# A hybrid decoder layer on one core: three small inputs loaded ahead of the modulation weights, the shift sum moved into a weight buffer, and one group's squares at earlier slices

## The chip, the cores and the metric

The kernel runs on one core of a Trainium2 chip. The metric is the device time of one execution in microseconds (us); lower is better. A core has five engines that run their own instruction streams side by side: TensorE (PE in the profile, with its weight loads shown apart as PEld), VectorE (DVE), ScalarE (ACT), GpSimd (POOL) and SyncE (SP). They wait for one another through semaphores. Transfers between memory and the core's buffers are issued by SP, ACT or POOL and carried out by 16 DMA engines. An instruction that waits holds up all that stands behind it on its engine, an issue of a transfer too.

## The reference

One decoder layer for 2048 tokens of width 1024. Cut to what matters here:

```
mod = silu(c) @ w_ada + b_ada              # c: 1024, w_ada: 1024 x 3072
shift, scale, gate = split(mod, 3)
h = rms_norm(x, g_pre) * (1 + scale) + shift        # x: 2048 x 1024
proj = h @ w_in
qa, ka, va, fa, za, qb, kb, vb, zb = split(proj)
oa = forgetting_attention(qa, ka, va, fa + b_fgate) * silu(za)      # 8 heads, causal
qb, kb = rope(qb, positions), rope(kb, positions)   # angle = position * inv_freq
ob = sliding_window_sink_attention(qb, kb, vb, sinks) * silu(zb)    # 8 heads, window 128
y = concat(oa, ob) @ w_out
x = x + gate * rms_norm(y, g_post)
```

Before any projection can start, the kernel needs `scale` and `shift`, that is two thirds of the product of `silu(c)` with 12 MB of `w_ada` (8 MB here), and the angles need `positions` and the 32 frequencies.

## The kernel before, in words

Tokens are worked in four groups of 512 (group `ci` = 0 to 3, `CH` = 512). A group is four x tiles of 128 rows (`xt0` to `xt15`, 512 KB each). For each tile the sum of squares is taken (`squares`, L421, on ACT for most tiles: one activation with a summing read), the inverse root for the group (`root`, L101 to L121), and the tile is scaled (`normal`, L433 on ACT for group 0, L435 on DVE for the others). `turn(ci, k)` transposes the 128 columns of slice k of a group's four tiles on PE (L441), applies scale and shift on ACT (`scaled`, L447, writes `hf` and for even k the high half), and DVE splits the result into two 16-bit halves of `hT` (`split`, L451 and L452). `hT[ci]` is the moving operand of the projections: `proj_units` (L353, keys kb, zb and others) and `vb_units` (L807). A projection's weights arrive raw (`wr_...`, L219 or L226, two buffers of tag `wraw`), and ACT and DVE turn them into a high half (`wh_...`, L271) and a low half (L277).

**The start block** (L470 to L692) is written out by hand, and its order on each engine is the order of the code. It loads `c`, `g_pre`, `b_ada`, `positions` and `inv_freq` (on ACT's queue), the 16 tiles `wa1k` (scale half) and `wa0k` (shift half) of `w_ada` (on SP's queue, L489, pool `wad` of 8 buffers), the first x tiles (L412), the raw weights `wr_kv` and `wr_zb1` (on POOL's queue) and `wr_zb0` (SP). The small rows are transposed into columns (L503, L506). The product of `silu(c)` with a half of `w_ada` is shared between PE and DVE: for most k PE multiplies a broadcast copy of `silu(c)` (`ada_pe`, L525), and for the others (1: k = 2, 4, 6; 0: k = 2, 4, 7) DVE accumulates `wa * sil` into `acc1` (scale) or `acc0` (shift) (`ada_dve`, L534 and L536), whose column sums PE adds with a matrix of ones; `ada_col` (L545) takes the diagonal out as columns. Between them, DVE computes angles for sine and cosine (`ang`, `kh`, L563 to L588), which begin with positions times `ifr`. The scaled shift and gain (`Gp`, `Shp`, L673 and L674) come last; after them the first `scaled` of group 0 can run, and with it the first projection. The rope tables are copied into place by SP (`spread`, L466 and L467), and then SP loads `xt8` and the tiles that follow.

**After the start block**, a list of units (`punits`) is emitted in order: for each group kb and vb, and for groups 0 to 2 a zb or va projection behind them. Every second unit is one slice; events bound to a slice (`at_slice`) are emitted ahead of it: the loads, squares, root and normal of the group that is two ahead, the turns of the next group (`at_` gives the places among the group's units), the weight halves. Outside the hand-ordered block, which of several independent instructions stands first on a queue is settled when the program is scheduled, not by one line of the code; the order shown below is what came out.

The lines that matter later: `wh_zb` (L271 on ACT) needs its place on ACT behind the squares of group 2; zb0's projection on PE needs `wh_zb` and its low half. The squares of group 3 stand, on ACT, ahead of the last turn's `hf` of group 2.

Of the kernel before, what the change touches and what calls it, by code (L numbers as in the profile page):

```python
# [10 lines left out]
F32 = mybir.dt.float32  # L11
# [32 lines left out]
def hybrid_layer(  # L44
# [17 lines left out]
    V, A, G, PE, SP = nc.vector, nc.scalar, nc.gpsimd, nc.tensor, nc.sync  # L62
# [20 lines left out]
    def sm(n, tag):  # L83
        return small.tile([P, n], F32, tag=tag, name=tag)
# [7 lines left out]
    def rsqrt_mean(dst, ss, n, eng=None):  # L92

        for _ in rsqrt_parts(dst, ss, n, eng=eng):
            pass
# [39 lines left out]
    wpool = right.enter_context(tc.tile_pool(name="wpool", bufs=2, side="right"))  # L135
# [19 lines left out]
    ident = const.tile([P, P], F32, name="ident")  # L155
# [26 lines left out]
    bk = [ps_bk.tile([P, CH], F32, name=f"bk{n}") for n in range(3)]  # L182
# [231 lines left out]
    def squares(ci, us=range(4), eng=None):  # L414
        if ci not in rstd:
            rstd[ci] = sm(4, "ss"), sm(4, "rst")
        for u in us:
            junk = hst.tile([P, D], BF16, tag="junk", name="junk", bufs=1)
            x_, sum_ = xt[ci * 4 + u], rstd[ci][0][:, u:u + 1]
            if eng is None:  # L420
                A.activation(junk[:], x_, AF.Square, accum_out=sum_)  # L421
            else:
                eng.scalar_tensor_tensor(junk[:], x_, 1.0, x_, op0=ALU.mult, op1=ALU.mult, accum_out=sum_)

    def root(ci):
        ss, rst = rstd[ci]
        rsqrt_mean(rst, ss[:], 4, G if ci else None)

    def normal(ci, us=range(4)):
        for u in us:  # L430
            t, r = ci * 4 + u, rstd[ci][1][:, u:u + 1]
            if ci == 0:
                A.activation(xt[t], xt[t], AF.Copy, scale=r)  # L433
            else:
                V.tensor_scalar(xt[t], xt[t], r, None, op0=ALU.mult)  # L435
# [20 lines left out]
    def turn_x(ci, k):  # L456
        scaled, split = turn(ci, k)
        after(1, scaled)
        after(2, split)

    def spread(g):

        gr, gc = slice(32 * g, 32 * g + 32), slice(g * CH, (g + 1) * CH)
        for r in range(4):
            rr = slice(32 * r, 32 * r + 32)
            SP.dma_start(cosT[rr, gc], cs_[gr, :])  # L466
            SP.dma_start(sinT[rr, gc], (sp_ if r % 2 else sn_)[gr, :])  # L467

    start = ExitStack()
    st = start.enter_context(tc.tile_pool(name="start", bufs=1, reuse_waits="tile"))  # L470
    wad = start.enter_context(tc.tile_pool(name="wad", bufs=8, reuse_waits="tile"))
    with tc.manual_schedule():
        rows = st.tile([P, P], F32, name="rows")
        posi = st.tile([4, CH], I32, name="posi")
        posf = st.tile([4, CH], F32, name="posf")
        sel = st.tile([4, 4, 32], F32, name="sel")
        ifr = st.tile([P, 1], F32, name="ifr")
        V.memset(rows[:], 0.0)
        V.memset(ones[:], 1.0)
        V.memset(lift[:], LIFT_A)  # L480
        A.dma_start(rows[0:8], c[0].rearrange("(k p) -> k p", p=P))
        A.dma_start(rows[8:16], g_pre[0].rearrange("(k p) -> k p", p=P))
        A.dma_start(rows[16:40], b_ada[0].rearrange("(k p) -> k p", p=P))
        A.dma_start(posi[:], positions[0].rearrange("(g n) -> g n", g=4))
        wa = {}

        def load_ada(half, k):
# [1 line left out]
            SP.dma_start(wa[half, k][:], w_ada0[k * P:(k + 1) * P, half * D:(half + 1) * D])  # L489


        A.dma_start(ifr[:], inv_freq)
        for k in range(KT):
            load_ada(1, k)
        for t in range(2):
# [4 lines left out]
        G.dma_start(bfg[:], b_fgate[0].partition_broadcast(P))  # L500
        V.tensor_copy(identb[:], ident[:])
        V.tensor_copy(identh[:], ident[:])
        PE.transpose(bk[0][:, :P], rows[:], ident[:])  # L503
        cols = st.tile([P, 40], F32, name="cols")
        V.tensor_copy(sel[:], ident[0:4, 0:4].unsqueeze(2).broadcast_to([4, 4, 32]))
        V.tensor_copy(cols[:], bk[0][:, :40])  # L506
        th = st.tile([P, KT], F32, name="th")
        A.activation(th[:], cols[:, 0:8], AF.Tanh, scale=0.5)
        hc = st.tile([P, KT], F32, name="hc")
        V.tensor_scalar(hc[:], cols[:, 0:8], 0.5, None, op0=ALU.mult)  # L510
# [7 lines left out]


        pm = {1: [ps_x.tile([P, CH], F32, tag="x", name="pm") for _ in range(2)], 0: [bk[1], bk[2]]}  # L520
        acc = [st.tile([P, D], F32, name=f"acc{n}") for n in range(2)]

        def ada_mm(half, lhsT, rows_, begin, end):
            for n in range(2):
                PE.matmul(pm[half][n][:], lhsT, rows_[:, n * CH:(n + 1) * CH], start=begin, stop=end)  # L525

        def ada_pe(half, k, begin=False, end=False):
            ada_mm(half, silb[:, k, :], wa[half, k], begin, end)

        def ada_dve(half, k, first_, parts=1):  # L530
            for n in range(parts):
                cc = slice(n * D // parts, (n + 1) * D // parts)
                if first_:
                    V.tensor_scalar(acc[half][:, cc], wa[half, k][:, cc], sil[:, k:k + 1], None, op0=ALU.mult)  # L534
                else:
                    V.scalar_tensor_tensor(acc[half][:, cc], wa[half, k][:, cc], sil[:, k:k + 1], acc[half][:, cc],  # L536
                                           op0=ALU.mult, op1=ALU.add)
# [25 lines left out]
        V.tensor_scalar(ang[:], bk[1][:], ifr[:], None, op0=ALU.mult)  # L563
# [26 lines left out]
        A.activation(sn_[:], sp_[:], AF.Copy, scale=-1.0)  # L590
        A.activation(dmask[:], dm32[:], AF.Copy)
        A.activation(dmaskT[:], dm32t[:], AF.Copy)

        def col8(name):
            return st.tile([P, KT], F32, name=name)


        for k in (0, 1, 3, 5, 7):
            ada_pe(1, k, k == 0)
        for k in (2, 4, 6):  # L600
            ada_dve(1, k, k == 2)
        for k in range(2):
# [25 lines left out]
        V.tensor_tensor(scl1[:], scl0[:], cols[:, 24:32], op=ALU.add)  # L628
        gcol = col8("gcol")
        V.scalar_tensor_tensor(gcol[:], scl1[:], 1.0, cols[:, 8:16], op0=ALU.add, op1=ALU.mult)  # L630
# [22 lines left out]
        shf0 = col8("shf0")  # L653
        ada_col(0, shf0)
        shf = col8("shf")
        V.tensor_tensor(shf[:], shf0[:], cols[:, 16:24], op=ALU.add)
# [315 lines left out]
    pkeys, punits = [], []  # L972
# [39 lines left out]
    def at_slice(n, f):  # L1012
        events.setdefault(n, []).append(f)
# [12 lines left out]
    for ci in range(NCH):  # L1026
        n0 = len(punits)
        add("kb", kb_units(ci))
        add("vb", vb_units(ci))
        if ci < 3:  # L1030
            add(*others[ci])
            if ci == 2:
                add(*others[4])
                add(*others[5])

            mine, punits[n0:] = punits[n0:], []
            at_ = ([14, 16, 17, 18, 19, 20, 21, 22], [8, 10, 12, 14, 16, 18, 20, 22], [18, 20, 22, 24, 26, 28, 30, 32])[ci]
            for n, u in enumerate(mine):
                punits.append(u)
                if n in at_:  # L1040
                    punits.append(lambda ci=ci, k=at_.index(n): turn_x(ci + 1, k))
            if ci < 2:

                for u in range(4):
                    at_slice(n0 + (28 if ci else 9) + u, lambda ci=ci, u=u: squares(ci + 2, (u,)))
                    at_slice(len(punits) + (10 if ci else -4) + u, lambda ci=ci, u=u: normal(ci + 2, (u,)))
                at_slice(len(punits) - (0 if ci else 18), lambda ci=ci: root(ci + 2))
            at_slice((12, 22, 30)[ci], lambda ci=ci: spread(ci + 1))
    n0 = len(punits)
    at_slice(n0, lambda: open_fox())  # L1050
# [742 lines left out]
```

## Time and profile before

| | us |
|---|---|
| median of 3 runs | 1155.18 (1154.89 to 1155.92) |
| the profiled execution | 1158.72, its span 1157.0 |
| PE busy | 1117.7 (97% of the span) |
| DVE busy | 929.3 (80%) |
| ACT busy | 660.3 (57%) |
| POOL busy | 209.1 (18%) |

The profiled execution lies 3.54 us above the median; its span leaves 1.7 us of it outside. PE is busy almost throughout, so its idle stretches and the stretches at a lower clock are where an edit of these lines can be seen. In the 40 slices of the profile (28.9 us each) PE shows 6 and 8 tenths in the first two and 9 or 10 tenths in nearly all of the others. Rows of a timeline give the start in us from the span's start, the duration, the engine (a q behind the name: its queue of waits and transfer issues), the line, the operation, output and inputs, how many instructions the row joins, and in brackets the idle time ahead of it and what ended that.

### The profile page before, as it was taken

What the parts mean: (1) busy time and instruction counts of PE and PEld (TensorE: products, weight loads), DVE (VectorE), ACT (ScalarE), POOL (GpSimd) and SP (SyncE); (2) the same over time, 40 slices, a digit from 0 to 9 for tenths busy, and PEclk for the clock granted to TensorE, in tenths of its full rate; (3) what the DMA queues carried; (4) which work ended last, traced back from release to release, by engine and by line L of the source; (5) the groups of instructions that cost most, each with busy time, mean ns of one, the idle gap of its engine ahead of it and who ended that gap; (6) DMA issues with size and microseconds to landing.
All of it is one profiled execution on the core that took longest, in us unless ns stands there. A gap on an engine that the chain in (4) does not pass through costs nothing. (4 is left out here: it accounts for less than half of the span.)

```text
span 1157.0 us, 25261 instructions
## 1 busy us (share of the span) xinstructions
PE 1117.7 (97%) x9853; PEld 654.9 (57%) x9853; DVE 929.3 (80%) x2149; ACT 660.3 (57%) x1148; POOL 209.1 (18%) x328
## 2 busy tenths in 40 slices
PE   6898999999999999999999999999999999999997
PEld 2476545577765865555555555555555555544444
DVE  6877468887878558788988899887898897778885
ACT  2776334655655521676757667666676778633332
POOL 1221124555556530010010101001000000000000
PEclk9999999999999999999999999999999999999999
DMA  9843345433232232443326332222311237687643
GB/s 341 308 127 70 79 82 100 96 58 88 61 86 94 57 82 58 63 104 49 82 61 83 90 62 59 53 49 70 53 40 36 78 92 220 138 221 204 196 142 109
DMA packets 123276, 119.84 MB, mean 104 GB/s; under 512 B 64872, under 2 KB 100752, under 8 KB 123156
## 3 DMA queue, kind: packets, MB, share of 16 engines
q1 hardware_dynamic: 112020, 85.67, 27.3%
q0 software_dynamic: 10816, 32.50, 13.3%
q8 instruction: 77, 1.26, 0.6%
q14 instruction: 43, 0.35, 0.2%
q10 hardware_dynamic: 320, 0.05, 0.0%
HBM read 64.49 MB, written 25.18 MB: 78 GB/s over the span
## 5 line engine op out<-in xcount | busy, mean ns | idle before, releaser
L1363 ACT ACTIVATE p<-sta,lift,scl_qk 128x1024 f32<-128x1024 f32 (+2 forms) x160 | 171.8, 1074 | 131.7 <-PE sta L1357 81.8
L353 PE MATMUL bk<-hT,wh_qk 128*128 128x512 f16 x768 | 194.7, 378 | 0.0
L1370 DVE TENSOR_TENSOR pha<-p,pha 128x1024 f16<-128x1024 f32 (+2 forms) x160 | 169.1, 1057 | 0.2 <-ACT pha L1367 0.2
L1310 DVE TENSOR_REDUCE a_m<-bk 128x1 f32<-128x512 f32 x192 | 130.4, 686 | 46.3 <-PE bk L1307 45.3
L1585 PE MATMUL bk<-wohl,oz 128*128 128x512 f16 x744 | 163.7, 379 | 1.1 <-DVE oz L1534 0.7
L1367 ACT ACTIVATE pha<-p 128x1024 f16<-128x1024 f32 (+2 forms) x160 | 148.1, 926 | 5.9 <-PE poa L1383 1.2
L1585 PEld LDWEIGHTS <-oz 128*128 128x128 f16 x744 | 70.6, 98 | 84.7 <-DVE oz L1534 1.8
L1383 PE MATMUL poa<-vt,pha 128*128 128x65 f16 x1088 | 116.1, 192 | 1.4 <-DVE pha L1370 1.4
L1380 PE MATMUL poa<-vt,pha 128*128 128x65 f16 x1088 | 116.6, 193 | 0.8 <-DVE ona L1389 0.7
L1382 PE MATMUL poa<-vt,pha 128*128 128x64 f16 x1088 | 116.6, 194 | 0.0
L353 PEld LDWEIGHTS <-wh_qk 128*128 128x128 f16 x768 | 72.1, 97 | 74.5 <-issue 2.1
L1356 PE MATMUL sta<-T 128*128 128x512 f16 (+1 forms) x320 | 110.9, 346 | 2.9 <-ACT p L1363 2.8
L1307 PE MATMUL bk<-T 66*128 66x512 f16 (+2 forms) x320 | 109.7, 348 | 2.9 <-DVE a_m L1310 1.9
L1380 PEld LDWEIGHTS <-pha 128*128 128x128 f16 x1088 | 101.5, 96 | 15.5 <-DVE ona L1389 1.9
L1357 PE MATMUL sta<-T 69*128 69x512 f16 (+1 forms) x320 | 109.8, 348 | 0.0
L1382 PEld LDWEIGHTS <-pha 128*128 128x128 f16 x1088 | 100.9, 97 | 11.4
L1383 PEld LDWEIGHTS <-pha 128*128 128x128 f16 x1088 | 100.8, 99 | 1.8 <-DVE pha L1370 1.8
L353 PE MATMUL bk<-hT,wh_za 128*128 128x512 f16 x384 | 99.7, 378 | 0.0
L353 PE MATMUL bk<-hT,wh_zb 128*128 128x512 f16 x384 | 92.1, 379 | 0.0
L371 PE MATMUL bk<-wh_va,hT 128*128 128x256 f16 x768 | 91.9, 273 | 0.0
L353 PE MATMUL bk<-hT,wh_qb 128*128 128x512 f16 x384 | 91.2, 379 | 0.0
L371 PEld LDWEIGHTS <-hT 128*128 128x128 f16 x768 | 73.3, 98 | 12.2 <-issue 2.1
(457 smaller groups left out, 1917.0 us busy)
## 6 DMA issues: line engine op xcount, KB each, us to landing
hT<-in_x_dram SPq DMA_DIRECT2D x20, 512.0 KB
wa<-in_w_ada_dram SPq DMA_DIRECT2D x16, 512.0 KB
z_d<-tz POOLq DMA_DIRECT2D x32, 256.0 KB, 3.0
T<-z_d SPq DMA_DIRECT2D x16, 512.0 KB
T<-stq SPq DMA_DIRECT2D x62, 128.0 KB
out_dram<-hT SPq DMA_DIRECT2D x15, 512.0 KB
xt<-in_x_dram SPq DMA_DIRECT2D x12, 512.0 KB
qs<-qf SPq DMA_DIRECT2D x80, 64.0 KB
```

The lines of the kernel that those rows point to most:

```text
L353: PE.matmul(ps, whl[:, a, k, :], hT[ci][:, b, k, :], start=(k == 0 and n == 0), stop=(k == KT - 1 and n == 2))
L371: PE.matmul(ps[:, (u % 2) * 2 * P:(u % 2 + 1) * 2 * P], hT[ci][:, a, k, u * P:(u + 1) * P], wv[p][:, b, k, :], start=(k == 0 and n == 0), ...
L1310: V.tensor_reduce(m3[:, u, pc:pc + 1], mx[:, :w], axis=AX.X, op=ALU.max)
L1356: PE.matmul(self.st[:, o:o + w], T[:, 3, kb_], T[:, 1, qc], start=True, stop=False)
L1357: PE.matmul(self.st[:, o:o + w], T[0:XR, 2, kb_], T[0:XR, 0, qc], start=False, stop=not diag)
L1363: A.activation(self.p32[:, :self.w], self.st[:, :self.w], AF.Exp, scale=scl[f"qk{self.hd}"][:], bias=lift[:])
L1367: A.activation(self.ph[:, 0, :self.w], self.p32[:, :self.w], AF.Copy)
L1370: V.tensor_tensor(self.ph[:, 1, :self.w], self.p32[:, :self.w], self.ph[:, 0, :self.w], op=ALU.subtract)
L1380: PE.matmul(po[:, u, :], ph[:, 0, pq], vt[:, b, hd, 0:65], start=(self.first and n == 0 and u == 0), stop=False)
L1382: PE.matmul(po[:, u, 0:64], ph[:, 0, pq], vt[:, b, hd, 65:VW], start=False, stop=False)
L1383: PE.matmul(po[:, u, :], ph[:, 1, pq], vt[:, b, hd, 0:65], start=False, stop=(self.last and n == len(self.blocks) - 1))
L1585: PE.matmul(py, self.hl[:, i, k, :], w_slot(8 * j + k)[:, cc], start=(k == 0 and m_ == 0), stop=(k == KT - 1 and m_ == 2))
```

## The change

1. `c`, `inv_freq` and `positions` are issued on SP ahead of the eight `wa1k` loads; `c` and `inv_freq` go into one small tile `rowc` (8 rows and 1 row), so the frequencies are one row of 128 numbers and no longer 128 partitions of one number. ACT keeps `g_pre` and `b_ada` (tile `rows`, now 32 rows).
2. `rowc` is transposed first; `rows` is transposed later, behind the first `ada_pe` of the scale half, into another buffer, and DVE copies it to `cols` behind the angles. The memset of `rows` is gone; one transpose and one copy are added.
3. `acc0` lies in the pool of raw weights (tag `wraw`, two buffers) and no longer in the start block's own pool.
4. Group 3's squares are bound to every second slice, 12 to 9 slices earlier than before, its root 7 slices and its normals 8 to 5 slices earlier, and the turns of group 3 stand two units earlier.

The diff, without the renumbered columns:

```diff
-        rows = st.tile([P, P], F32, name="rows")
+        rows = st.tile([32, P], F32, name="rows")
+        rowc = st.tile([KT + 1, P], F32, name="rowc")
...
-        A.dma_start(rows[0:8], c[0].rearrange("(k p) -> k p", p=P))
-        A.dma_start(rows[8:16], g_pre[0].rearrange("(k p) -> k p", p=P))
-        A.dma_start(rows[16:40], b_ada[0].rearrange("(k p) -> k p", p=P))
-        A.dma_start(posi[:], positions[0].rearrange("(g n) -> g n", g=4))
+        SP.dma_start(rowc[0:KT], c[0].rearrange("(k p) -> k p", p=P))
+        SP.dma_start(rowc[KT:KT + 1], inv_freq.rearrange("p o -> o p"))
+        SP.dma_start(posi[:], positions[0].rearrange("(g n) -> g n", g=4))
...
-        A.dma_start(ifr[:], inv_freq)
+        A.dma_start(rows[0:8], g_pre[0].rearrange("(k p) -> k p", p=P))
+        A.dma_start(rows[8:32], b_ada[0].rearrange("(k p) -> k p", p=P))
...
-        PE.transpose(bk[0][:, :P], rows[:], ident[:])
+        PE.transpose(bk[0][:, 0:KT + 1], rowc[:], ident[0:KT + 1, 0:KT + 1])
...
-        acc = [st.tile([P, D], F32, name=f"acc{n}") for n in range(2)]
+        acc = [wpool.tile([P, D], F32, tag="wraw", name="acc0"), st.tile([P, D], F32, name="acc1")]
...
+        ada_pe(1, 0, True)
+        PE.transpose(bk[2][:, 0:4 * KT], rows[:], ident[0:32, 0:32])
...
-        V.tensor_scalar(ang[:], bk[1][:], ifr[:], None, op0=ALU.mult)
+        V.tensor_scalar(ang[:], bk[1][:], colc[:, KT:KT + 1], None, op0=ALU.mult)
...
+        V.tensor_copy(cols[:], bk[2][:, 0:4 * KT])
...
-            at_ = (..., [18, 20, 22, 24, 26, 28, 30, 32])[ci]
+            at_ = (..., [16, 18, 20, 22, 24, 26, 28, 30])[ci]
...
-                    at_slice(n0 + (28 if ci else 9) + u, lambda ci=ci, u=u: squares(ci + 2, (u,)))
-                    at_slice(len(punits) + (10 if ci else -4) + u, lambda ci=ci, u=u: normal(ci + 2, (u,)))
-                at_slice(len(punits) - (0 if ci else 18), lambda ci=ci: root(ci + 2))
+                    at_slice(n0 + (16 + 2 * u if ci else 9 + u), lambda ci=ci, u=u: squares(ci + 2, (u,)))
+                    at_slice(len(punits) + (2 + 2 * u if ci else u - 4), lambda ci=ci, u=u: normal(ci + 2, (u,)))
+                at_slice(len(punits) - (7 if ci else 18), lambda ci=ci: root(ci + 2))
```

**On SP, at the end of the start block.** `cosT` and `sinT` are the rope tables' copies, `xt8` to `xt11` the x tiles of group 2, `xt12` to `xt15` those of group 3. Before:

```order
L467 DMA sinT_112<-sp__235 32x512
L412 DMA xt8_531<-in_x_dram 128x1024
L412 DMA xt9_533<-in_x_dram 128x1024
L412 DMA xt10_535<-in_x_dram 128x1024
L412 DMA xt11_537<-in_x_dram 128x1024
L412 DMA xt12_572<-in_x_dram 128x1024
L412 DMA xt13_574<-in_x_dram 128x1024
L412 DMA xt14_576<-in_x_dram 128x1024
L412 DMA xt15_578<-in_x_dram 128x1024
L763 DMA qs_604<-qf_603 32x512 x4
```

The same place on SP after the change:

```order
L467 DMA sinT_112<-sp__238 32x512
L412 DMA xt12_574<-in_x_dram 128x1024
L412 DMA xt13_576<-in_x_dram 128x1024
L412 DMA xt14_578<-in_x_dram 128x1024
L412 DMA xt15_580<-in_x_dram 128x1024
L412 DMA xt8_533<-in_x_dram 128x1024
L412 DMA xt9_535<-in_x_dram 128x1024
L412 DMA xt10_537<-in_x_dram 128x1024
L412 DMA xt11_539<-in_x_dram 128x1024
L767 DMA qs_606<-qf_605 32x512 x4
```

The eight loads are the same; group 3's tiles now stand ahead of group 2's, which moved from places 1 to 4 to places 5 to 8.

**On ACT, in group 1's slices.** `L447` rows are turns of group 2 (`hT2` the high half, `hf` the full one), `L421` the squares of group 3's tiles, `vb` (L815, L819) an output of the vb projection, `stb` a rope result, `tz` a gate. Before, from the second vb output to the gate of zb1:

```order
L815 ACTIVATE vb_566<-bk0_136 128x2x64 x2
L780 ACTIVATE stb_936<-qc_935 128x512
L447 ACTIVATE hT2_109<-px_1087,Shp_115,Gp_114 128x512
L447 ACTIVATE hf_1092<-px_1087,Shp_115,Gp_114 128x512
L447 ACTIVATE hf_1118<-px_1113,Shp_115,Gp_114 128x512
L447 ACTIVATE hT2_109<-px_1126,Shp_115,Gp_114 128x512
L447 ACTIVATE hf_1131<-px_1126,Shp_115,Gp_114 128x512
L421 ACTIVATE junk_1138,ss_1136<-xt12_572 128x1024
L421 ACTIVATE junk_1143,ss_1136<-xt13_574 128x1024
L421 ACTIVATE junk_1149,ss_1136<-xt14_576 128x1024
L421 ACTIVATE junk_1157,ss_1136<-xt15_578 128x1024
L447 ACTIVATE hf_1156<-px_1151,Shp_115,Gp_114 128x512
```

After, from the second of the squares (that of `xt12` stands directly ahead) to the last turn's `hf`:

```order
L421 ACTIVATE junk_1067,ss_1038<-xt13_576 128x1024
L447 ACTIVATE hf_1074<-px_1069,Shp_115,Gp_114 128x512
L819 ACTIVATE vb_568<-bk0_136 128x2x64 x2
L421 ACTIVATE junk_1092,ss_1038<-xt14_578 128x1024
L784 ACTIVATE stb_938<-qc_937 128x512
L447 ACTIVATE hT2_109<-px_1097,Shp_115,Gp_114 128x512
L447 ACTIVATE hf_1102<-px_1097,Shp_115,Gp_114 128x512
L421 ACTIVATE junk_1111,ss_1038<-xt15_580 128x1024
L447 ACTIVATE hf_1130<-px_1125,Shp_115,Gp_114 128x512
L447 ACTIVATE hT2_109<-px_1161,Shp_115,Gp_114 128x512
L447 ACTIVATE hf_1166<-px_1161,Shp_115,Gp_114 128x512
L447 ACTIVATE hf_1183<-px_1178,Shp_115,Gp_114 128x512
```

The four squares no longer stand in one block ahead of the last turn's `hf`; they are spread between earlier turns, so the last `hf` follows the turn before it directly.

**On POOL, at the end of its part of the start block.** `dm`, `dm32t` and `triu` are masks, `wr_zb1` the raw weights of zb1, `rs_t` the first step of an inverse root. Before, with the waits that rows carry:

```order
L556 AFFINE_SELECT dm32t_214<-zero_208 128x128
L558 AFFINE_SELECT triu_124<-ones_125 128x128
L219 DMA wr_zb1_595<-in_w_in_dram 128x8x128
L114 TENSOR_TENSOR rs_t_476<-rs_y_472 128x4 [waits DVE_49]
L115 TENSOR_TENSOR rs_t_476<-rs_t_476,rs_v_470 128x4 [waits Pool_49]
```

After:

```order
L559 AFFINE_SELECT dm32t_217<-zero_211 128x128
L561 AFFINE_SELECT triu_124<-ones_125 128x128
L219 DMA wr_zb1_597<-in_w_in_dram 128x8x128 [waits DVE_49,PE_49]
L114 TENSOR_TENSOR rs_t_478<-rs_y_474 128x4 [waits DVE_49]
L115 TENSOR_TENSOR rs_t_478<-rs_t_478,rs_v_472 128x4 [waits Pool_49]
```

The row keeps its place, but the load of `wr_zb1` now goes into the buffer that holds `acc0`, and waits for the last reader of that, the shift's column sums.

More of the change, by code (lines that the diff above doesn't have):

```diff
@@ L476, in hybrid_layer @@
         sel = st.tile([4, 4, 32], F32, name="sel")
-        ifr = st.tile([P, 1], F32, name="ifr")
-        V.memset(rows[:], 0.0)
         V.memset(ones[:], 1.0)
         V.memset(lift[:], LIFT_A)
-        A.dma_start(rows[0:8], c[0].rearrange("(k p) -> k p", p=P))
-        A.dma_start(rows[8:16], g_pre[0].rearrange("(k p) -> k p", p=P))
-        A.dma_start(rows[16:40], b_ada[0].rearrange("(k p) -> k p", p=P))
-        A.dma_start(posi[:], positions[0].rearrange("(g n) -> g n", g=4))
+        SP.dma_start(rowc[0:KT], c[0].rearrange("(k p) -> k p", p=P))
+        SP.dma_start(rowc[KT:KT + 1], inv_freq.rearrange("p o -> o p"))
+        SP.dma_start(posi[:], positions[0].rearrange("(g n) -> g n", g=4))
         wa = {}
@@ L502, in hybrid_layer @@
         V.tensor_copy(identh[:], ident[:])
-        PE.transpose(bk[0][:, :P], rows[:], ident[:])
-        cols = st.tile([P, 40], F32, name="cols")
+        PE.transpose(bk[0][:, 0:KT + 1], rowc[:], ident[0:KT + 1, 0:KT + 1])
+        colc = st.tile([P, KT + 1], F32, name="colc")
+        cols = st.tile([P, 32], F32, name="cols")
         V.tensor_copy(sel[:], ident[0:4, 0:4].unsqueeze(2).broadcast_to([4, 4, 32]))
-        V.tensor_copy(cols[:], bk[0][:, :40])
+        V.tensor_copy(colc[:], bk[0][:, 0:KT + 1])
         th = st.tile([P, KT], F32, name="th")
-        A.activation(th[:], cols[:, 0:8], AF.Tanh, scale=0.5)
+        A.activation(th[:], colc[:, 0:8], AF.Tanh, scale=0.5)
         hc = st.tile([P, KT], F32, name="hc")
-        V.tensor_scalar(hc[:], cols[:, 0:8], 0.5, None, op0=ALU.mult)
+        V.tensor_scalar(hc[:], colc[:, 0:8], 0.5, None, op0=ALU.mult)
         V.tensor_copy(posf[:], posi[:])
@@ L592, in hybrid_layer @@
         A.activation(dmaskT[:], dm32t[:], AF.Copy)
+        V.tensor_copy(cols[:], bk[2][:, 0:4 * KT])
         def col8(name):
             return st.tile([P, KT], F32, name=name)
-        for k in (0, 1, 3, 5, 7):
-            ada_pe(1, k, k == 0)
+        for k in (1, 3, 5, 7):
+            ada_pe(1, k)
         for k in (2, 4, 6):
@@ L627, in hybrid_layer @@
         scl1 = col8("scl1")
-        V.tensor_tensor(scl1[:], scl0[:], cols[:, 24:32], op=ALU.add)
+        V.tensor_tensor(scl1[:], scl0[:], cols[:, 16:24], op=ALU.add)
         gcol = col8("gcol")
-        V.scalar_tensor_tensor(gcol[:], scl1[:], 1.0, cols[:, 8:16], op0=ALU.add, op1=ALU.mult)
+        V.scalar_tensor_tensor(gcol[:], scl1[:], 1.0, cols[:, 0:8], op0=ALU.add, op1=ALU.mult)
         absg = col8("absg")
@@ L655, in hybrid_layer @@
         shf = col8("shf")
-        V.tensor_tensor(shf[:], shf0[:], cols[:, 16:24], op=ALU.add)
+        V.tensor_tensor(shf[:], shf0[:], cols[:, 8:16], op=ALU.add)
         abss = col8("abss")
@@ L1036, in hybrid_layer @@
             mine, punits[n0:] = punits[n0:], []
-            at_ = ([14, 16, 17, 18, 19, 20, 21, 22], [8, 10, 12, 14, 16, 18, 20, 22], [18, 20, 22, 24, 26, 28, 30, 32])[ci]
+            at_ = ([14, 16, 17, 18, 19, 20, 21, 22], [8, 10, 12, 14, 16, 18, 20, 22], [16, 18, 20, 22, 24, 26, 28, 30])[ci]
             for n, u in enumerate(mine):
```

## The prediction

> **What bounds the kernel now.** I read the page's engine rows first. The profiled execution took 1158.72 us, 1157.0 of it in the span:
>
> ```profile
> span 1157.0 us, 25261 instructions
> PE 1117.7 (97%) x9853; PEld 654.9 (57%) x9853; DVE 929.3 (80%) x2149; ACT 660.3 (57%) x1148; POOL 209.1 (18%) x328
> ```
>
> PE is the bound: 39 us of the span are idle, and nearly everything that an edit of these lines can give lies there or in stretches at a lower clock. The list of PE's waits between 50 and 130 us, where the edited slices are, comes next, and begins with (engine, line, what was waited for, us in total, times, longest):
>
> ```profile
> PE bk L353 <- DVE hT L451: 2.6, 1, 2.6
> ```
>
> That is a single wait. The timelines of PE, ACT and DVE around it:
>
> ```profile
> 93.70 2.11 PE L353 MATMUL bk<-hT,wh_kb 128*128 128x512 f16 x9
> 98.38 0.38 PE L353 MATMUL bk<-hT,wh_kb 128*128 128x512 f16 x1 [2.57 <-DVE hT L451]
> 99.10 0.59 PE L353 MATMUL bk<-hT,wh_kb 128*128 128x512 f16 x2 [0.35 <-DVE hT L452]
> ```
>
> ```profile
> 92.45 1.07 ACT L421 ACTIVATE junk<-xt 128x1024 bf16<-128x1024 f32 x1
> ...
> 97.06 0.76 ACT L447 ACTIVATE hf<-px,Shp,Gp 128x512 f32<-128x512 f32 x1
> ```
>
> ```profile
> 97.85 0.47 DVE L451 CAST hT<-hf 128x512 f16<-128x512 f32 x1
> ```
>
> From 92.45 to 97.06 ACT takes the four squares of group 3 in one block; the last `hf` of group 2 stands behind them, so DVE's cast starts at 97.85 and PE, which ran out of work at 95.81, resumes at 98.38. The windows show what follows, and the same thing earlier in the start block (bounds, length, busy times and counts, PEclk, DMA share, GB/s):
>
> ```profile
> 25.10:28.50 3.40, 3.40 (x6) 1.15 (x6) 2.92 (x11) 1.32 (x4) 0.00 (x0) 0.50 1.02 408
> ...
> 100.20:103.60 3.40, 3.40 (x34) 3.40 (x32) 2.12 (x6) 1.63 (x2) 2.60 (x8) 0.50 0.16 64
> ```
>
> ```profile
> 20.87 1.98 PE L525 MATMUL pm<-wa,silb 128*128 128x512 f32 x4 [1.12 <-DMA wa<-in_w_ada_dram]
> ...
> 24.83 3.55 PE L525 MATMUL pm<-acc,ones 128*128 128x512 f32 x4 [1.98 <-DVE acc L536]
> ```
>
> Here a wait of 2.57 us, and one of 1.98, are each followed by 3.4 us at half clock (a loss of 1.7 us of matmul work), while 1.12 us at 20.87 is not. So the stall at 96 us costs 2.57 + 0.35 + 1.7 = 4.62 us.
>
> **The start block.** These rows carry its chain:
>
> ```profile
> 1.08 0.60 ACTq L481 DMA_DIRECT2D rows<-in_c_dram  x1
> ...
> 2.05 0.31 ACTq L483 DMA_DIRECT2D rows<-in_b_ada_dram  x1
> 2.39 0.32 ACTq L484 DMA_DIRECT2D posi<-in_positions_dram  x1
> 2.74 0.92 ACTq L492 DMA_DIRECT2D ifr<-in_freq_dram  x1
> ```
>
> ```profile
> 7.17 0.45 PE L503 MATMUL bk<-ident,rows 128*128 128x128 f32 x1 [7.17 <-DMA rows<-in_b_ada_dram]
> ...
> 12.27 0.75 DVE L563 TENSOR_SCALAR ang<-bk,ifr 128x512 f32<-128x512 f32 x1 [2.95 <-DMA ifr<-in_freq_dram]
> ```
>
> ```profile
> 34.58 3.70 PE L525 MATMUL bk<-wa,silb 128*128 128x512 f32 x8 [0.30 <-DMA wa<-in_w_ada_dram]
> ```
>
> ```profile
> 38.74 1.41 DVE L536 SCALAR_TENSOR_TENSOR acc<-wa,sil,acc 128x512 f32<-128x512 f32 x2
> ...
> 45.09 0.23 DVE L673 TENSOR_SCALAR Gp<-gcol,ipH 128x8 f32<-128x8 f32 x1
> ```
>
> DVE loses 2.95 us on the frequencies, and its last accumulation into the shift sum starts at 38.74; `Gp` follows 6.35 us later, then the first projection. In the new order the angles need `c`, frequencies and positions alone, at the head of SP's queue. The transpose at 7.17 waited for `b_ada`, 5.1 us behind that load's issue at 2.05. If SP's third small load is issued near 1.7 and takes as long, the transpose starts near 6.8; `ang` came 5.1 us behind the transpose, 2.95 of it the wait, so I put it at 9.0 (bounds 7.0, a shorter landing, and 12.27, no gain): 3.3 us off DVE's chain. The sum is then not DVE's to set. At 34.58 PE waits, by its place in the order, for `wa05`; `wa06` and `wa07` come behind it in the same stream, each 524 KB at 408 GB/s (the window at 25.10), 1.28 us: `wa07` lands near 37.1, so about 1.6 us are to be had. The stream itself moves: three issues ahead of it (0.60 for `c`, 0.32 for positions, 0.3 to 0.92 for the frequencies, nearest to 0.3 since it is one row now: about 1.2 us) delay it, and `wr_zb1`, which shared it, leaves (1.28 us earlier); together −0.1, bounds −1.3 to +1.2. I take the last accumulation, `Gp` and the first projection 1.7 us earlier (bounds 0.4 and 2.9). The added transpose and copy hide: both stand where PE and DVE wait for `w_ada` (the wait ahead of 20.87 is one); without that cover each costs less than half a microsecond (0.45 for the old transpose, 0.47 for the cast at 97.85).
>
> **What that gain meets.** SP, POOL, ACT and PE between the start block and zb0:
>
> ```profile
> 10.12 0.92 POOL L219 DMA_DIRECT2D wr_zb<-in_w_in_dram  x1
> ```
>
> ```profile
> wr_zb<-in_w_in_dram POOLq DMA_DIRECT2D x1, 512.0 KB, 9.6
> ```
>
> ```profile
> 44.87 0.51 SPq L467 DMA_DIRECT2D sinT<-sp__235  x1
> 47.41 0.82 SPq L412 DMA_DIRECT2D xt<-in_x_dram  x2
> ```
>
> ```profile
> 59.76 1.06 ACT L421 ACTIVATE junk<-xt 128x1024 bf16<-128x1024 f32 x1
> 60.71 0.20 ACT L421 ACTIVATION_READ_ACCUMULATOR junk<-xt 128x1 f32 x1
> 60.80 1.14 ACT L271 ACTIVATE wh_zb<-wr_zb,w_sw 128x1024 f16<-128x1024 f32 x1
> ```
>
> ```profile
> 62.19 0.98 PE L353 MATMUL bk<-hT,wh_zb 128*128 128x512 f16 x3
> ```
>
> ```profile
> 47.40:50.00 2.60, 1.90 (x9) 0.71 (x8) 2.50 (x9) 2.60 (x5) 1.47 (x3) 1.00 0.56 187
> 50.00:52.50 2.50, 2.29 (x10) 0.86 (x9) 2.38 (x5) 2.50 (x5) 2.17 (x5) 1.00 0.90 329
> 52.50:55.00 2.50, 1.79 (x8) 0.65 (x7) 2.28 (x5) 1.18 (x2) 2.12 (x5) 1.00 1.00 393
> 55.00:57.50 2.50, 2.50 (x36) 2.25 (x36) 2.46 (x7) 1.92 (x4) 0.20 (x1) 1.00 1.02 413
> 57.50:60.00 2.50, 2.33 (x41) 2.21 (x38) 2.40 (x9) 2.47 (x7) 0.00 (x0) 1.00 1.02 385
> 60.00:62.00 2.00, 2.00 (x32) 1.85 (x30) 1.28 (x6) 2.00 (x4) 0.00 (x0) 1.00 0.66 148
> 62.00:64.00 2.00, 2.00 (x17) 1.19 (x14) 1.93 (x6) 1.96 (x5) 0.63 (x1) 1.00 0.23 55
> ```
>
> Before, SP starts the x tiles at 47.41 with group 2's first. Group 2's squares end at 60.8, and `wh_zb` of zb0 and all else of ACT follow. Now group 3's four tiles go ahead, and `xt11`, the last square's input, is eighth. When does an eighth tile land? Eight tiles are 4.19 MB; the window rates add up to 4.28 MB by 60.0, and traffic of them runs on into the last windows: between 59.8 and about 63.0, middle 61.4. The start moves: the old order waited at 47.41 for the transposes of `xt0`, the new one goes straight behind `sinT`, which issues when `wr_zb0` has landed (44.87 + 0.51 = 45.4, and the 0.1 of the stream: 45.3). But `wr_zb1` is now issued when the shift's columns are read, close by, and takes 1.28 us of the transfers: I give half of it to `wr_zb0`, so the x tiles start at 45.9, 1.5 us earlier, and half to the x tiles. `xt11`: 61.4 − 1.5 + 0.6 = 60.5; its square 1.04 (59.76 to 60.80); `wh_zb` at 61.5, 0.7 later than before (bounds: 58.1 + 1.04 when ACT itself sets it, 59.1; and with no earlier start and all of `wr_zb1` ahead, 63.0 + 1.28 + 1.04 = 65.3).
>
> That rests on how the queues share. The POOL load before took 9.6 us for 512 KB in a full stream, 55 GB/s, much less than an equal part.
>
> The Trainium skill ("DMA: Bandwidth & Descriptors", section on queues, rings and completion order) says that each DMA engine takes turns between the queue rows that have work, packet by packet. By that, `wr_zb1` would take an equal turn and cost `wr_zb0` nearly the whole 1.28 us, 0.6 us more in the sum. The 9.6 us speak against an equal turn here.
>
> So the 1.7 us do not come out at zb0: PE would be there at 62.19 − 1.7 = 60.5 and waits till 62.9, 2.4 us, which by the two rows above halves the clock once more (−1.7 of work, as much as goes at 100 us). PE is then 0.7 + 1.7 = 2.4 us late. Part comes back in group 1's turn slices, where PE waits for DVE:
>
> ```profile
> 75.25 0.81 PE L353 MATMUL bk<-hT,wh_kb 128*128 128x512 f16 x3 [0.39 <-DVE hT L452]
> ...
> 76.32 0.59 PE L353 MATMUL bk<-hT,wh_kb 128*128 128x512 f16 x2 [0.26 <-DVE hT L452]
> ```
>
> A later PE swallows them: −0.65.
>
> **The slices of groups 1 and 2.** With the squares spread, ACT takes one (1.26 us with its read) between turns; the last `hf` no longer stands behind four, and 4.62 us go. What is late next is a turn behind one square: by the two small waits just quoted, 0.2 us in all, bounds 0 and 0.8. The squares' data landed 30 us before. The earlier root and normals run on POOL and DVE, and group 3's turns two units earlier find normals that are 8 to 5 slices earlier: nothing, bounds −0.4 to +0.4.
>
> **Sum.** +0.7 (wh_zb) + 1.7 (half clock at zb0) − 0.65 − 4.62 + 0.2 = −2.7 us. 1158.72 − 2.7 = 1156.0 for a profiled execution, which lies 3.54 above the median; against that, 1155.18 − 2.7 = **1152.5**. The half clock stands in it twice with opposite signs, so its size hardly matters. The case's own bounds: 1150.8 without a half clock at zb0, 1153.7 with 0.8 for the small waits and `wr_zb1` wholly ahead of `wr_zb0` (0.6).
>
> **Rivals.**
> 1. *The x tiles come in time.* `xt11` lands by 58.1 (4.19 MB from 45.9 at 400 GB/s would end at 56.4), ACT never waits, and all 1.7 us stay: −1.7 − 4.62 + 0.2 = −6.1, 1149.1. For it: the rates of the full windows; against it: the slow first window (187 GB/s) and the tail to 63. Of these two only the tail shows the tiles themselves. Beside this, the Trainium skill ("TensorE: Matmul & The Clock Gate", part on the HAM clock gate) says that the half clock comes after an idle window of about 3.4 us. By that the half clock at 100 us would not be the 2.57 us wait's doing and would stay: −4.4, 1150.8. The waits of 1.98 and 2.57 us followed by 0.50 speak against it.
> 2. *The spread squares make waits of their own.* Each sits ahead of a turn that PE needs soon; the two waits at 75 and 76 us show that DVE's halves come with nothing to spare. If half of 4.62 returns: −0.4, 1154.8.
> 3. *Slower: group 2's tiles are too late.* `xt11` lands at 63.0 + 1.28 = 64.3, `wh_zb` starts 4.5 us later. Then 4.5 + 1.7 − 0.65 − 4.62 + 0.2 = +1.1, and since PE's wait of 4.5 + 1.7 = 6.2 us is twice as long as any above, and ACT's turns of group 1 stand behind it too, a second half-clock stretch: +2.8, 1158.0. It decides from `wh_zb` 3.4 us late, at 64.2. For it: places 5 to 8; against it: SP's earlier start.
> 4. *The start is bound elsewhere and the slices too:* nothing moves, 1155.2.
>
> **How the numbers follow.** What a measurement can tell from no change is about 0.2%, 2.3 us: the borders are 1152.9 and 1157.5. Main case 0.43, of which 0.27 below 1152.9 and 0.16 above. Rival 1: 0.19, faster. Rival 2: 0.16, the same. Rival 3: 0.18, of which 0.13 slower and 0.05 the same. Rival 4: 0.04, the same. Faster 0.27 + 0.19 = 0.46; same 0.16 + 0.16 + 0.05 + 0.04 = 0.41; slower 0.13. The range takes in the main case, rival 2 and the better parts of 1 and 3, and leaves out about a tenth at each end: 1148.8 to 1157.2.
>
> **What would show it.** Right: `ang` near 7 us; `Gp` near 43.4; x tiles issued near 46; ACT waiting for `xt` at 55 to 60; `wh_zb` near 61.5 with a wait of PE for it and half clock behind; no wait over 0.5 us at 96 us and no half clock at 100. Wrong: `wh_zb` before 60 (rival 1) or after 64 (rival 3); a row of waits for `hT` between 78 and 98 us (rival 2); `Gp` not earlier, so the stream, not DVE, set it.

## The result and the profile after

The changed kernel takes 1151.55 us (median of 6 runs, 1151.14 to 1152.51), the kernel before 1155.65 (1154.89 to 1159.14, 6 runs); the ratio is 0.9961, 95% interval 0.9948 to 0.9974, that is 4.5 us less (3.0 to 6.0). The profiled execution took 1151.27 us. Its page, the span and the engines:

```profile
span 1149.5 us, 25258 instructions
PE 1117.5 (97%) x9854; PEld 653.9 (57%) x9854; DVE 930.4 (81%) x2149; ACT 660.2 (57%) x1148; POOL 211.1 (18%) x328
```

PE's waits between 50 and 130 us:

```profile
PE bk L353 <- DVE hT L452: 1.3, 4, 0.4
PE px L441 <- DVE hT L435: 0.3, 1, 0.3
PE bk L353 <- ACT wh_zb L271: 0.3, 1, 0.3
PE bk L353 <- DVE wh_zb L277: 0.2, 1, 0.2
PE bk L811 <- DVE mxs L1022: 0.2, 1, 0.2
```

The wait of 2.6 us for the last turn of group 2 is gone, and two small ones for `wh_zb` are new. PE's timeline through kb and vb of group 2, and the windows over that vb:

```profile
89.68 5.34 PE L353 MATMUL bk<-hT,wh_kb 128*128 128x512 f16 x24
94.86 5.84 PE L811 MATMUL bk<-wh_vb,hT 128*128 128x136 f16 x96
100.53 0.81 PE L353 MATMUL bk<-hT,wh_zb 128*128 128x512 f16 x3
```

```profile
94.80:98.20 3.40, 3.40 (x59) 3.34 (x57) 2.85 (x9) 1.24 (x2) 1.86 (x4) 1.00 0.36 89
98.20:100.60 2.40, 2.40 (x44) 2.40 (x42) 2.40 (x5) 0.73 (x3) 0.00 (x0) 1.00 0.74 221
```

All 24 matmuls of kb stand in one row, and the clock behind them is 1.00 where it was 0.50. From the first of them to zb1 it is 100.53 − 89.68 = 10.85 us; before it was 106.84 − 91.11 = 15.73. Before, the first projection, the first kb matmul of group 2 and zb1 stood at:

```profile
46.38 0.38 PE L353 MATMUL bk<-hT,wh_kb 128*128 128x512 f16 x1 [0.92 <-ACT hT L447]
...
91.11 4.70 PE L353 MATMUL bk<-hT,wh_kb 128*128 128x512 f16 x21
...
106.84 2.10 PE L353 MATMUL bk<-hT,wh_zb 128*128 128x512 f16 x9
```

After the change, the start block on PE, DVE, SP and ACT:

```profile
2.80 0.24 PE L502 MATMUL bk<-ident,rowc 9*128 9x9 f32 x1 [2.80 <-DMA rowc<-in_freq_dram]
```

```profile
5.93 0.75 DVE L566 TENSOR_SCALAR ang<-bk,colc 128x512 f32<-128x512 f32 x1 [1.21 <-PE bk L513]
...
35.77 1.41 DVE L539 SCALAR_TENSOR_TENSOR acc<-wa,sil,acc 128x512 f32<-128x512 f32 x2
...
42.53 0.23 DVE L677 TENSOR_SCALAR Gp<-gcol,ipH 128x8 f32<-128x8 f32 x1
```

```profile
1.84 4.10 SPq L487 DMA_DIRECT2D wa<-in_w_ada_dram  x8
...
43.24 0.51 SPq L467 DMA_DIRECT2D sinT<-sp__238  x1
43.96 5.00 SPq L412 DMA_DIRECT2D xt<-in_x_dram  x8
```

```profile
55.08 1.06 ACT L421 ACTIVATE junk<-xt 128x1024 bf16<-128x1024 f32 x1 [0.20 <-DMA xt<-in_x_dram]
...
58.33 1.06 ACT L421 ACTIVATE junk<-xt 128x1024 bf16<-128x1024 f32 x1 [0.49 <-DMA xt<-in_x_dram]
...
59.38 1.13 ACT L271 ACTIVATE wh_zb<-wr_zb,w_sw 128x1024 f16<-128x1024 f32 x1
```

```profile
43.82 0.38 PE L353 MATMUL bk<-hT,wh_kb 128*128 128x512 f16 x1 [0.92 <-ACT hT L447]
...
60.57 0.61 PE L353 MATMUL bk<-hT,wh_zb 128*128 128x512 f16 x2 [0.31 <-ACT wh_zb L271]
```

The first projection starts at 43.82 (46.38 before), zb0 at 60.57 (62.19): 2.56 us are gained and 0.94 given back, where ACT waits for two of group 2's tiles. The two spans differ by 7.5 us, the timed runs by 4.1 to 4.5: so the pair of profiles says too much, and the question for the experiments was which of the two parts the time comes from.

### The profile page after: what moved, and what is told of

Read it like the earlier page. It is cut to its first block, busy times and chain, and to the rows that moved or that the text cites. A ratio compares the mean times of both kernels' runs of the same rounds, so it can differ in the third digit from the quotient of the medians.

```text
span 1149.5 us, 25258 instructions
## 1 busy us (share of the span) xinstructions
PE 1117.5 (97%) x9854; PEld 653.9 (57%) x9854; DVE 930.4 (81%) x2149; ACT 660.2 (57%) x1148; POOL 211.1 (18%) x328
```

## The experiments

Four marks in PE's timeline tell the runs apart: the first kb matmul (A), the first of zb0 (B), the first kb matmul of group 2 (C) and the first of zb1 (D). In us, one profile each. The ratio is the time over that of the kernel before on the same chip, with its 95% interval. e0 to e3, e4 to e7 and e8 to e10 ran on three different chips, so between these groups the ratios compare better than the medians.

| kernel | A | A to B | C to D | median us | ratio (95%) |
|---|---|---|---|---|---|
| before, first profile | 46.38 | 15.81 | 15.73 | 1155.65 | |
| before again (e0) | 44.64 | 15.82 | 15.44 | 1156.45 | 0.9999 (0.9988 to 1.0009) |
| changed | 43.82 | 16.75 | 10.85 | 1151.55 | 0.9961 (0.9948 to 0.9974) |
| squares only (e1) | 44.12 | 15.82 | 11.04 | 1152.02 | 0.9962 (0.9947 to 0.9978) |
| start block only (e2) | 43.28 | 17.25 | 15.00 | 1156.72 | 1.0003 (0.9991 to 1.0016) |
| group 3's loads behind slice 12 (e3) | 43.10 | 15.82 | 16.86 | 1155.94 | 1.0000 (0.9989 to 1.0010) |
| acc0 back (e4) | 44.02 | 15.85 | 11.55 | 1150.87 | 0.9958 (0.9945 to 0.9971) |
| pools swapped (e5) | 43.29 | 15.82 | 11.28 | 1149.38 | 0.9947 (0.9933 to 0.9961) |
| turns back (e6) | 44.76 | 17.53 | 10.86 | 1151.62 | 0.9968 (0.9957 to 0.9979) |
| small loads on ACT (e7) | 41.86 | 15.81 | 11.38 | 1147.91 | 0.9934 (0.9921 to 0.9947) |
| one square early (e8) | 44.05 | 15.82 | 13.02 | 1154.06 | 0.9982 (0.9973 to 0.9990) |
| two squares early (e9) | 44.33 | 15.82 | 11.83 | 1152.45 | 0.9963 (0.9951 to 0.9976) |
| e4 with small loads on ACT (e10) | 43.71 | 15.85 | 11.15 | 1150.05 | 0.9946 (0.9933 to 0.9960) |

**The kernel before, again.** No edit.

> The kernel before, unchanged, for a second profile of it. The first pair of profiles differs by 7.4 us at the end, the timed runs by 4.1. Theory A: what lies between them is in the one profiled execution of before, which had waits or half-clock stretches that most executions lack; then this profile's span is nearer to 1153.5 than to 1157.0, and the rows that shrink are the half clock at 100.2 (1.7 us) or the wait near 210 to 250 (1.3 us). Rival B: the profiled execution of before is typical and the changed kernel loses 3 us in other executions; then this span is 1156 to 1158 again. Time against before: ratio 1.000.

Its profile has a span of 1154.7, and its first kb matmul and the stall are:

```profile
44.64 0.38 PE L353 MATMUL bk<-hT,wh_kb 128*128 128x512 f16 x1 [0.91 <-ACT hT L447]
...
96.74 1.74 PE L353 MATMUL bk<-hT,wh_kb 128*128 128x512 f16 x3 [2.66 <-DVE hT L451]
98.27 6.72 PE L807 MATMUL bk<-wh_vb,hT 128*128 128x136 f16 x96
```

The stall and the half clock are there again (vb takes 6.72 us, at full clock 5.84). What the first profile had more was neither of them: 1.74 of the 2.3 us by which this profile is shorter lie ahead of the first projection. There the first profile has the half clock at 25.10 that the prediction shows, and the column sums of the scale (24.83, also shown there) take 3.55 us. In this profile the clock is not halved there, and they take 1.99:

```profile
23.59 1.99 PE L525 MATMUL pm<-acc,ones 128*128 128x512 f32 x4
```

So theory A held in its span and in its kind, a half-clock stretch that other executions lack, but not in its place. The start of an unchanged block varies: 46.38, 44.64, and 44.12, 44.05, 44.33 in the three kernels below that keep it; only the first of the five has a half clock in it.

**The squares alone.** The kernel before with part 4 of the change.

> The kernel before with part 4 alone (group 3's squares, root and normals earlier, turns two units earlier); the start block is the old one. Theory A: the stall at 96 us (2.92 us) goes in every execution and the half clock behind it where there is one (1.7): 2.9 to 4.6 us faster, and this is most of the whole change. Rival B, the spread squares make waits of their own between 78 and 98 us: under 2 us faster.

1152.02 us, ratio 0.9962: as much as the whole change. C to D falls by 4.4 to 4.7 us, and no wait stands in it:

```profile
88.87 5.34 PE L353 MATMUL bk<-hT,wh_kb 128*128 128x512 f16 x24
...
99.91 0.81 PE L353 MATMUL bk<-hT,wh_zb 128*128 128x512 f16 x3
```

Theory A held, near the upper end of its range.

**The start block alone.** The changed kernel with the old slices for squares, root, normals and turns.

> The changed kernel with part 4 undone: new start block, old squares. Theory A: the first projection is 2.5 us earlier, 1.1 us of it is given back at zb0 where ACT waits for group 2's tiles, and the stall at 96 us stays: 1.4 us faster than before, and its parts add up with the squares alone. Rival B: the start block gives nothing in time, or the stall grows by what PE is earlier: 0, and the sum of the two parts alone is over or under the whole by more than 1 us.

1.0003 (0.9991 to 1.0016): no gain that these runs can tell. PE's row at zb0, and ACT's squares ahead of it:

```profile
60.53 0.60 PE L353 MATMUL bk<-hT,wh_zb 128*128 128x512 f16 x2 [0.48 <-ACT wh_zb L271]
```

```profile
53.51 1.06 ACT L421 ACTIVATE junk<-xt 128x1024 bf16<-128x1024 f32 x1 [0.46 <-DMA xt<-in_x_dram]
54.85 1.06 ACT L421 ACTIVATE junk<-xt 128x1024 bf16<-128x1024 f32 x1 [0.20 <-DMA xt<-in_x_dram]
...
58.29 1.06 ACT L421 ACTIVATE junk<-xt 128x1024 bf16<-128x1024 f32 x1 [0.66 <-DMA xt<-in_x_dram]
```

A to B is 17.25 us here, 16.75 and 17.53 in the other two profiles of that x order, and 15.81 to 15.85 in all ten of the old one. Rival B held in the time, but its second mark did not come: by their ratios the two parts alone add up to 4.1 us, the whole is 4.5. In the profiles, what the start gains (A is 43.65 in the mean of the five profiles with small loads on SP and a late `wr_zb1`, 44.70 in the five of the old block) goes at zb0. This profile is of one of the fastest of its twelve executions (1154.75 us, their median 1156.72), so it does not show what the others lose.

**Group 2's tiles first, by a later event.**

```
-    at_slice(1, lambda: [load_x(t) for t in range(12, 16)])
+    at_slice(12, lambda: [load_x(t) for t in range(12, 16)])
```

> The changed kernel, with the loads of group 3's tiles bound to slice 12 where it was slice 1, so that SP loads xt8 to xt11 ahead of xt12 to xt15 as before the change; acc0 stays in the weights' buffer and wr_zb1 late. Theory A: ACT no longer waits for xt (0.2 and 0.5 us before the squares of xt9 and xt11) and wh_zb comes up to 1.1 us earlier: 0.7 to 1.1 us faster than the changed kernel. Rival: zb0 is set by something else that is just behind (the low half on DVE, or the transposes of group 1), 0 to 0.4 us.

zb0 is as far behind A as before (15.82), but the whole gain of the squares is lost: 1155.94. DVE and SP show why:

```profile
88.49 0.69 DVE L780 TENSOR_TENSOR qs<-qs,sinT 128x512 f32<-128x512 f32 x1 [7.78 <-DMA qs<-qf]
```

```profile
SPq L767 <- ACT qf L765: 5.9, 1, 5.9
SPq L467 <- DMA xt<-in_x_dram: 2.8, 1, 2.8
SPq L466 <- DMA xt<-in_x_dram: 0.8, 1, 0.8
```

Group 3's loads now stand behind the rope transfers of group 0 (`qs`), which wait for ACT, and the table copies behind them wait for the tiles. SP comes to the `qs` transfers of group 1 at 80.10 where the changed kernel has 76.13; DVE, which has them ahead of its splits, stands till 88.49 (85.06), the last turns are late, and PE waits four times:

```profile
90.30 0.38 PE L353 MATMUL bk<-hT,wh_kb 128*128 128x512 f16 x1 [0.36 <-DVE hT L451]
91.02 0.81 PE L353 MATMUL bk<-hT,wh_kb 128*128 128x512 f16 x3 [0.35 <-DVE hT L452]
92.76 0.81 PE L353 MATMUL bk<-hT,wh_kb 128*128 128x512 f16 x2 [0.94 <-DVE hT L452]
94.16 4.30 PE L353 MATMUL bk<-hT,wh_kb 128*128 128x512 f16 x9 [0.59 <-DVE hT L451]
```

Neither theory had this. Nine matmuls take 4.30 us in the last row, and 2.11 at full clock; the window over them has PEclk 0.50:

```profile
94.00:97.50 3.50, 3.20 (x8) 1.06 (x8) 3.19 (x6) 2.20 (x4) 2.95 (x7) 0.50 0.49 119
```

**acc0 back.** `acc` is again two tiles of `st`; the rest as changed.

> The changed kernel with acc0 in the start block's own pool again: wr_zb1 is loaded early on POOL as before, and SP loads xt8 to xt11 first. Theory A (the late wr_zb1 takes 1.28 us out of the w_ada stream; its price is the swap of the x tiles, which costs zb0 1 us or more): without both, wa07 lands 1.3 us later and zb0 gets no wait for x tiles: about the changed kernel's time, within 1 us. Rival B, the early small loads carry the start block's gain and the stream is not the limit: the first projection stays as early as in the changed kernel (44.5) and zb0 is 1 us earlier: 1 us faster than it.

With `acc0` back the x order goes back too, so the move of `acc0` is what swapped the tiles. A is 44.02, only 0.4 later than the mean of the five with a late `wr_zb1`; zb0 loses nothing; 1150.87, 0.3 us below the changed kernel by the ratios and 0.7 by the medians. That is within the 1 us of theory A, but one profile whose A is 0.4 and not 1.3 later does not set it apart from rival B.

The late `wr_zb1` has a price on the way to the first projection too, which no theory had: its issue on POOL (0.92 us, at 40.10 in the changed kernel) overlaps DVE's `dgb` (L669, L665 in the kernel before). That step takes 0.68 or 0.69 us in the six profiles with a late `wr_zb1` and 0.28 or 0.29 in the other seven, and PE's wait behind it is 0.80 and 0.40. Why the two disturb each other was not looked into.

**The pools swapped.**

```
-            xt[t] = (xlate["pool"] if t >= 12 else xin).tile(...)
+            xt[t] = (xlate["pool"] if 8 <= t < 12 else xin).tile(...)
```

with the two `load_x` loops exchanged.

> The changed kernel with the two groups of x tiles exchanged between their buffers: group 2's tiles take the buffers that are free early and group 3's the late ones, so that SP loads xt8 to xt11, then xt12 to xt15, in one go. Theory A (the change's x order costs 0.7 us of ACT's waits and 1.1 to 1.6 us at zb0, and the loss of the run with group 3's loads behind slice 12 came from its SP queue, not from group 2 being first): zb0 starts near 59.2, no wait returns at 85 to 98: 1 to 2 us faster than the changed kernel, 5 to 6 us faster than before. Rival B (PE being early at zb0 only moves a wait to the rope of group 1, whose DVE steps wait for the transfers of qs): 0 to 0.5 us faster.

ACT's squares of group 2 no longer wait:

```profile
52.96 1.05 ACT L421 ACTIVATE junk<-xt 128x1024 bf16<-128x1024 f32 x1
...
56.69 1.05 ACT L421 ACTIVATE junk<-xt 128x1024 bf16<-128x1024 f32 x1
57.73 1.14 ACT L271 ACTIVATE wh_zb<-wr_zb,w_sw 128x1024 f16<-128x1024 f32 x1
```

1149.38 us, 6 below the kernel before. Below the changed kernel it is 1.6 by the ratios, whose intervals overlap, and 2.2 by the medians; e6, on the same chip and the changed kernel but for its turns, has 1151.62. That is theory A, by the ratios inside its 1 to 2 and by the medians a little over. This profile has a half clock too, behind the first projection, and it costs nothing (A to B is 15.82 as in the others):

```profile
45.72:49.12 3.40, 3.13 (x8) 1.02 (x7) 3.28 (x7) 3.40 (x7) 3.06 (x5) 0.50 1.00 396
```

DVE and ACT are busy for 3.28 and 3.40 of these 3.40 us, and in the changed kernel's profile, at full clock, PE waits for DVE in the same stretch (0.35, 0.21 and 0.32 us).

**The turns back.** The old `at_` numbers in the changed kernel.

> The changed kernel with group 3's turns two units later again (the old at_ numbers); squares, root and normals stay early. Theory A: the turns have nothing to do with the stall at 96 us: same time within 0.5 us. Rival: the earlier turns feed the kb projection of group 3 in time: 0.5 to 1.5 us slower.

1151.62, the same by the medians and 0.8 us slower by the ratios, which is less than their intervals can tell: that does not decide between theory A and the rival. The stall did not come back (C to D is 10.86). Its start happened to be late (A 44.76).

**The small loads on ACT.** The pools swapped, and `c`, the frequency row and positions issued by ACT ahead of `g_pre` and `b_ada`.

> The run with the pools swapped, and c, the frequency row and positions issued first on ACT, ahead of g_pre and b_ada, where the change has them on SP: the w_ada stream starts 1.05 us earlier (0.79 against 1.84). Theory A (the stream of w_ada and x sets the start block): wa07 lands up to 1 us earlier, the first projection too, 0.5 to 1 us faster than with the pools swapped. Rival B (the stream loses nothing at its head, since the first tile's landing is not waited for and the transfers are full later anyway): within 0.3 us.

1147.91 us, the fastest of all. The first kb matmul:

```profile
41.86 0.38 PE L353 MATMUL bk<-hT,wh_kb 128*128 128x512 f16 x1 [0.92 <-ACT hT L447]
```

It is 1.43 us earlier than with these loads on SP (one profile each), and the time is 1.5 us shorter on the same chip: theory A, over its 0.5 to 1. So the head of SP's queue was not free: the 1.05 us by which `w_ada` starts later in the changed kernel is paid.

**One and two squares early.** The kernel before, with only the first one or two of group 3's squares at the new slices.

> The kernel before with only the first of group 3's four squares at its early slice; three stand in a block ahead of the last turn's hf. Each square takes 1.19 us of ACT. Theory A (the stall is the block's length, and the half clock comes behind a wait of about 2 us or more, not behind 1.1): the wait of PE shrinks from 2.6 to about 1.4 us and the half clock behind it goes: 2.5 to 3.5 us faster than before. Rival B (the half clock has another cause than that wait, for instance its place in a grid of time): the wait shrinks by 1.2 and the half clock stays: 1.2 us faster.

> The kernel before with the first two of group 3's squares early, two left in a block. Theory A: the wait shrinks to 0.2 to 0.4 us, no half clock: 4 to 4.6 us faster than before, as much as with all four early. Rival B: 2.4 us faster, with a half-clock window still to be seen near 100 us.

PE's rows with one early, and the windows over them:

```profile
94.98 0.38 PE L353 MATMUL bk<-hT,wh_kb 128*128 128x512 f16 x1 [1.49 <-DVE hT L451]
95.70 0.59 PE L353 MATMUL bk<-hT,wh_kb 128*128 128x512 f16 x2 [0.35 <-DVE hT L452]
96.14 5.84 PE L807 MATMUL bk<-wh_vb,hT 128*128 128x136 f16 x96
```

```profile
95.00:96.10 1.10, 0.75 (x3) 0.27 (x3) 1.10 (x2) 0.05 (x1) 0.87 (x2) 1.00 0.00 0
96.10:99.50 3.40, 3.40 (x58) 3.36 (x57) 2.04 (x8) 1.96 (x4) 2.47 (x11) 1.00 0.02 5
```

A wait of 1.49 us leaves the clock at 1.00 in this profile; C to D falls by 2.4 to 2.7 us for one square of 1.19. Two squares early bring C to D to 11.83. The granted clock of whole executions agrees: its median is 0.998 over e8's eleven and 0.997 over the fifteen of the kernel before on the same chip, and 3.4 us at half clock take 0.0015 off such a mean. Theory A held in the trace. In time e8 gives 2.1 us (1.2 to 3.1), a little under theory A's range and not apart from rival B's 1.2; e9's 4.3 (2.8 to 5.7) is theory A's.

**acc0 back with the small loads on ACT.** e4 with the loads of e7.

> The run with acc0 back, and c, the frequency row and positions first on ACT's queue: early small loads, early squares, but wr_zb1 early and x order as before. Against the run with small loads on ACT and the pools swapped it differs by wr_zb1's place (and the tiles' buffers). Theory A (wr_zb1's 512 KB cost the w_ada stream 1.28 us): 1 to 1.5 us slower than that run. Rival B (the stream has gaps that take it in, since it waits for buffers): within 0.4 us of it, so the move of acc0 was not needed.

A is 1.85 us later than in e7, the time 1.4 us longer by the ratios (2.1 by the medians, of two chips): theory A, though their intervals overlap. In e4 against e5, with the loads on SP, A differs by 0.7. The 1.28 us of `wr_zb1`'s bytes lie between the two; with one profile each and a start that varies by half a microsecond and more, its price is not known closer than that.

## Why the prediction was right, and where it was not

The forecast was −2.7 us, the result −4.5 (3.0 to 6.0), inside the range. By its steps:

- **The stall** (4.62 removed, 0.2 put back). Measured 4.4 to 4.9 from C to D and −4.4 us in time for this part alone. Right in place and size. That the half clock hangs on the wait was argued from two rows; in e8's profile the wait is 1.49 and the half clock is gone. Rival 2 (waits between the spread squares) did not come.
- **`ang` at 9.0**, measured 5.93, under the bound: the first transpose starts at 2.80, not near 6.8, since `c` and the frequencies have landed by then. It made no difference, as the prediction said: ahead of the shift's column sums PE now waits for `wa` (1.16 and 0.57 us), not for DVE.
- **The first projection 1.7 us earlier.** 2.56 in the pair of profiles, 1.05 between the means of five and five. The start block of the kernel before varies by over 2 us, and the profile that carried the sum was its slowest of five: the half clock at 25.10, which the prediction quotes only to price the one at 100 us, was in that start block too, and the other four profiles lack it.
- **What the gain meets.** The x order did take it back: A to B is 0.9 to 1.7 us longer with it. The prediction had zb0 0.7 us later than before. In the pair of profiles it is 1.62 earlier; in the mean it is 61.13 (the three profiles with the new x order and small loads on SP) against 60.52 (the five of the old block), 0.6 later. But the last tile came earlier than 60.5: ACT's wait for it ended at 58.33, 14.4 us after the first issue at 43.96, where the prediction had 14.6 us after 45.9. So the length was right and the start 1.9 us off, 1.5 of it because SP came to `sinT` at 43.24, where the prediction left it at 44.77; `wh_zb` came at 59.38, not at 61.5.
- **The half clock at zb0, +1.7, is the term that failed.** It needed one wait of 2.4 us, till 62.9. With `wh_zb` 2.1 us earlier than forecast, all that PE gave back by zb0 was 0.94 us, and its waits there were 0.34, 0.31 and 0.18: the first is at group 1's transposes, for a DVE step that stands behind an ACT output between the late squares. No half clock followed at zb0 in any of the three profiles of that x order. Without this term the sum is −4.4, the measured value but for 0.1; that it fits so closely is partly luck, since two other terms were off as well. The −0.65 for later waits did not come either: group 1's two waits are still there,

```profile
73.82 0.81 PE L353 MATMUL bk<-hT,wh_kb 128*128 128x512 f16 x3 [0.38 <-DVE hT L452]
74.88 0.59 PE L353 MATMUL bk<-hT,wh_kb 128*128 128x512 f16 x2 [0.25 <-DVE hT L452]
```

and A to C grew by 1.1 us (45.86 against 44.73), no less than A to B. The other is one that the prediction did not have, the stretch behind D (below).

So the whole gain that the times show is the squares'; the start block as changed is worth nothing that they can tell (1.0003). By the first projections of these profiles that is, as an estimate, a gain of about a microsecond for each of two edits (early frequencies and late `wr_zb1`; no run has the frequencies alone) against 0.9 to 1.7 at zb0 and the 1.05 us at SP's head.

Two things stay open. Beyond the half clock of the first profile, why the start block varies from execution to execution is not known. And from D to the end of the last matmul it is 1042.1 to 1042.8 us in the five profiles with the old start block and 1040.1 to 1041.2 in the eight with a new one. PE's waits for `sm_`, the exponentials of the window attention on ACT (L923, L927 in the changed kernel), add up to 1.6 to 2.7 us between 130 and 260 us in those five and to 0.3 to 1.1 in those eight. So the profiles have a gain of 1 to 2 us far behind the start block that goes with it. What makes it, and why e2's time shows none of it, no run says.

## What to carry to other kernels

A block of work for a later group, put on an engine ahead of the last instruction that the present group needs, costs its length as a wait, less the work that the waiting engine still has, and, if the wait is long, a slow clock behind it; spreading half of it was as good here as spreading all. When a buffer is moved, look at every queue's order afterwards: here one accumulator's new place swapped eight loads, and that took back about what the edit gained. A single profile of a start that waits on transfers can be two microseconds off; repeat it before its rows carry a sum.

## What was not expected of the hardware

Three waits of 0.36, 0.35 and 0.94 us within 2.8 us (e3) were followed by the half clock, at 93.0, as a single one of 2.3 to 2.7 us was, while 1.49 with 0.35 behind it (e8) was not. So short waits can do it together, but their sum does not decide alone. The waits of 0.92, 0.29 and 0.29 us at the first projection are about the same in every profile, and a half clock follows them in three (e4, e5, e10, at 46.35, 45.72 and 45.93) and not in the other ten. What may decide is where the waits fall: within a trace, the changes of the clock lie whole multiples of 3.41 us apart (first profile: 25.10, 28.51, 100.20, 103.61; e4: 15.63, 19.05, 46.35, 49.77). That is read from the traces, and not tested by itself; by it, part of what e8 shows could be its place on such a grid.

The first tile of `w_ada` starting 1.05 us later moved the first projection 1.43 us, although in both profiles the transfers are busy from 3 us on (a DMA share of 0.94 or more in every window up to 40 us).
